# The first projection blocks of a transformer layer, put in written order, with four channel blocks of their modulation multiplied on TensorE

## The chip, the cores and the metric

The kernel runs on one core of a Trainium2 chip. The metric is the device time in microseconds (us) of one execution, from launch to the end on the chip; the time of a kernel is the median of its runs. A core has TensorE (PE in the rows), VectorE (DVE), ScalarE (ACT), GpSimd (POOL), a sequencer that issues transfers (SyncE, SP in the rows), and 16 DMA engines.

## The reference

One decoder layer on a sequence of 2048 positions with 1024 channels, in float32. A condition vector gives six vectors of 1024 numbers, the modulation; each sub-layer normalises its input, scales and shifts it by the modulation, and adds its result through a gate. Of what follows the projection only the names matter here: four heads of gated linear attention, eight heads of dilated attention, an output projection, a feed-forward part with a convolution of width 3.

```python
cond = jax.nn.silu(c)
mod = (cond @ w_ada[l] + b_ada[l])[:, None, :]
sh1, sc1, g1, sh2, sc2, g2 = jnp.split(mod, N_MOD, axis=-1)
h = rms_norm(x, norm1_g[l]) * (1 + sc1) + sh1
proj = h @ w_in[l]
gq, gk, gv, gr, glr, aq, ak, av = jnp.split(proj, split_at, axis=-1)
...
x = x + g1 * (mixed @ w_out[l])
h = rms_norm(x, norm2_g[l]) * (1 + sc2) + sh2
u = causal_depthwise_conv(h @ w_up[l], conv_w[l], conv_b[l])
x = x + g2 * ((jax.nn.silu(u_gate) * u_val) @ w_down[l])
```

## The kernel before

The sequence is worked in four chunks of 512 positions, the 1024 channels in eight blocks of 128, one on the partitions each. Every large product is done as three float32r matmuls (`mm3`): both factors are split into a high part and the rest, and high by high, high by rest and rest by high are added up in PSUM (lines 288, 289 and 290; which of the two factors is the stationary one depends on the product). Weights arrive by DMA as `wraw`; ScalarE rounds them to `whi` (line 226) and VectorE subtracts to get `wlo` (line 227). The normalised input `x` is multiplied by `G` and `rstd` on VectorE (line 415), ScalarE adds the shift and rounds to `hhi` (line 417), and VectorE forms `hlo` (line 419). `rstd` comes from a sum of squares: a matmul with a matrix of equal numbers (`ones`, line 402), then a logarithm and an exponential on ScalarE (`norm_end`).

The modulation is 48 blocks of 128 numbers. A block is one row of 1024 weights on each partition (`wada`, 512 KB), multiplied by the condition and added up along the row on VectorE (line 326); then the bias is added (line 332) and, for a scale, `G` is formed (line 336). Channel block k of the first input needs two of them, the scale 8+k and the shift k. The first 16 blocks are fetched and multiplied at the start; the other 32 by `ada_late`, between other work (line 355).

The start goes as follows. The input of chunk 0 is fetched, `rstd` is formed, and for each channel block k its two modulation blocks are multiplied and `h0[k]` is formed. The first four output blocks of the projection, `FIRST`, have a PSUM tile each, to which channel block k can be added as soon as `h0[k]` and the weights are there: 4 x 8 x 3 = 96 matmuls of 128x512. Then comes the projection's next block, V0 (moving rows 272 wide), and the rest in the order of `ORDER0`: `g0 g1 g2 g3 V0 q0 q1 W0 q2 q3 V1 q4 q5 q6 q7 W1`. W1 is a block of four `wide` steps; ScalarE and VectorE turn its four PSUM tiles into `stg` (lines 496 and 497), and `stg` frees the tiles. Weights for the later blocks, the late modulation and the statistics of the next chunk (`stats`: eight loads, squares and sums, then `norm_end`) are laced into the projection by counting steps (`along`), and the mixing of chunk 0 (`mix(0)`) starts 27 steps later. A compiler pass with a timeline of its own sorts each engine's instructions, so that the order on an engine is not that of the code where nothing pins it. Loads of constants, the input of chunk 1 and the late modulation wait for a chosen instruction (`gate_ins`, `after`), here the modulation of k = 6 (`GATE`).

Of the kernel before, what the change touches and what calls it, by code (L numbers as in the profile page):

```python
# [26 lines left out]
GATE = 6  # L27
# [103 lines left out]

class K:
# [19 lines left out]
    def cload(self, name, shape, dt=F32):  # L152
        t = self.const.tile(list(shape), dt, name=name + "_sb")
        self.nc.sync.dma_start(t, self.A[name])
        return t

# [18 lines left out]
    def consts(self):  # L175
        nc, A = self.nc, self.A
        self.ct = self.const.tile(list(CONSTS.shape), F32, name="consts_sb")
        self.after(nc.sync.dma_start(self.ct, A["consts"]))
        self.mk = self.cload("masks", MASKS.shape, U32)
# [6 lines left out]
        nc.vector.tensor_scalar(self.qgs, self.C("qsc"), self.qg[:, 0:1], -0.5, op0=ALU.mult, op1=ALU.mult)  # L186
        self.kgs = self.const.tile([P, 1], F32, name="kgs")
        nc.vector.tensor_scalar(self.kgs, self.kg, -0.5, None, op0=ALU.mult)
        self.gw = self.const.tile([17, 256], F32, name="gw")
        nc.sync.dma_start(self.gw[0:16], A["gla_w_gate"])  # L190
        nc.sync.dma_start(self.gw[16:17], A["gla_b_gate"])
        self.gB = self.const.tile([P, 4, P], F32, name="gB")
        g = A["gla_norm_g"]
        nc.sync.dma_start(self.gB, bass.AP(tensor=g.tensor, offset=g.offset, ap=[[0, P], [0, 4], [1, P]]))
        nc.vector.tensor_scalar(self.gB, self.gB, 0.5, None, op0=ALU.mult)
        self.blk = self.const.tile([P, P], F32R, name="blk")
        nc.vector.tensor_copy(self.blk, self.C("blk"))
# [95 lines left out]
    def ada_setup(self):  # L293
        nc, c = self.nc, self.A["c"]
        self.cond = self.const.tile([P, 1024], F32, name="cond")
        nc.sync.dma_start(self.cond, bass.AP(tensor=c.tensor, offset=c.offset, ap=[[0, P], [1, 1024]]))
        self.n1 = self.cload("norm1_g", [P, KD])
        self.n2 = self.cload("norm2_g", [P, KD])
# [30 lines left out]
    def ada_end(self, b):  # L329
# [3 lines left out]
        for j, G, g in ((1, self.G1, self.n1), (4, self.G2, self.n2)):  # L333
            if b // KD == j:
                k = b % KD
                nc.vector.scalar_tensor_tensor(G[:, k:k + 1], m, 1.0, g[:, k:k + 1], op0=ALU.add, op1=ALU.mult)
# [641 lines left out]

    def run(self):
        self.ada_setup()  # L980
        self.scratch()
        self.x1, self.h2, self.tail = {}, {}, ()
        self.planned = False
# [5 lines left out]
        for k in range(KD):  # L989
# [3 lines left out]
            for g in gs:  # L993
                next(g)
# [81 lines left out]
def colv(v):  # L1076
    return v.reshape(-1, P).T
# [37 lines left out]
```

## Time and profile before

| | us |
|---|---|
| median of 3 runs | 2643.39 |
| lowest and highest run | 2640.31, 2644.96 |
| the profiled execution, its own time | 2639.45 |
| span of the profiled execution, first to last instruction | 2637.7 |

The profiled execution took 1.75 us more than its span, and 3.94 us less than the median. Rows of the trace give times from the start of the span. In a row of a timeline the first number is the start of an instruction, the second its length; matmuls overlap, so that the distance of two starts is shorter than a length. In square brackets stands the idle time of the engine before it and what ended it.

### The profile page before, as it was taken

To read this page: it belongs to the slowest core of one execution; us is meant where nothing else is said; L and a number is where in the kernel's file an instruction comes from. 1 tells how busy PE (TensorE), PEld (TensorE's weight loads), DVE (VectorE), ACT (ScalarE), POOL (GpSimd) and SP (SyncE) were. 2 spreads that over 40 slices of the span, in tenths; PEclk is the share of its full clock that TensorE was granted. 3 is DMA by queue.
4 is the path that set the end of the run, shared out by engine and by line. 5 is a ranking of instruction groups with operands and counts; after the bars stand their busy time and mean duration, and the time that the engine had idled before them with its cause. 6 is when DMAs were issued, how large, how long until landed. Compare 5 with 4: busy or idle time off the path is not lost.

```text
span 2637.7 us, 46896 instructions
## 1 busy us (share of the span) xinstructions
PE 2575.8 (98%) x18152; PEld 2114.0 (80%) x18152; DVE 1921.7 (73%) x4120; ACT 1276.3 (48%) x2607; POOL 243.8 (9%) x460
## 2 busy tenths in 40 slices
PE   5999999999989999999999999999999999999999
PEld 4878888788768888888788888878888888788887
DVE  7577886758677776776887777778778766666665
ACT  4556556656445444553545445345455443433332
POOL 0111101101000000000000000000000000010010
PEclk9999999999989999999999999999999999999999
DMA  8766565756623343446434444643344445332222
GB/s 290 256 201 226 189 230 182 231 177 204 225 81 104 98 124 127 126 151 218 140 102 128 136 133 138 199 164 111 112 149 129 136 133 182 134 104 96 96 96 88
DMA packets 192640, 405.10 MB, mean 154 GB/s; under 512 B 19985, under 2 KB 70946, under 8 KB 191138
## 3 DMA queue, kind: packets, MB, share of 16 engines
q0 software_dynamic: 60992, 220.49, 25.8%
q1 hardware_dynamic: 131426, 181.62, 21.0%
q8 instruction: 143, 2.34, 0.4%
q14 instruction: 79, 0.65, 0.1%
HBM read 339.12 MB, written 62.91 MB: 152 GB/s over the span
## 4 chain that ended last, share of the span: by engine, by line
PE 88%; DVE 4%; DMA 4%; ACT 2%; issue 1%; SPq 0%; POOL 0%; DVEq 0%; ACTq 0%; POOLq 0%
PE psg L288 26%; PE psg L289 25%; PE psg L290 25%; PE psa L757 2%; PE psa L737 2%; PE psa L859 2%; DMA wada<-in_w_ada_dram 1%; PE psa L595 1%; DVE wlo L227 1%; DMA x<-x 1%; PE psa L773 1%; PE psa L854 1%; PE psa L666 1%; DMA sq<-in_xT_dram 1%; PE psa L665 1%
## 5 line engine op out<-in xcount | busy, mean ns | idle before, releaser
L288 PE MATMUL psg<-hhi,whi 128*128 128x512 f32 x2040 | 807.5, 398 | 16.5 <-ACT hhi L417 8.6
L289 PE MATMUL psg<-hlo,whi 128*128 128x512 f32 x2040 | 804.9, 395 | 2.4 <-DVE hlo L419 2.4
L290 PE MATMUL psg<-hhi,wlo 128*128 128x512 f32 x2040 | 803.6, 394 | 0.9 <-DVE wlo L227 0.9
L226 ACT CAST whi<-wraw 128x1024 fp32r<-128x1024 f32 (+1 forms) x391 | 410.3, 1050 | 492.7 <-PE psg L289 422.4
L227 DVE TENSOR_TENSOR wlo<-wraw,whi 128x1024 fp32r<-128x1024 f32 (+1 forms) x391 | 478.8, 1225 | 186.6 <-ACT whi L226 179.8
L288 PEld LDWEIGHTS psg<-hhi,whi 128*128 128x128 f32 x2040 | 386.0, 189 | 104.6 <-ACT hhi L417 10.7
L290 PEld LDWEIGHTS psg<-hhi,wlo 128*128 128x128 f32 x2040 | 385.9, 189 | 83.9 <-DVE wlo L227 2.1
L289 PEld LDWEIGHTS psg<-hlo,whi 128*128 128x128 f32 x2040 | 386.1, 189 | 83.6 <-DVE hlo L419 3.5
L288 PE MATMUL psg<-ghi,whi 128*128 128x512 f32 x704 | 279.6, 398 | 0.0
L289 PE MATMUL psg<-glo,whi 128*128 128x512 f32 x704 | 277.3, 394 | 0.0
L290 PE MATMUL psg<-ghi,wlo 128*128 128x512 f32 x704 | 276.1, 392 | 0.0
L971 DVE SCALAR_TENSOR_TENSOR x<-psg,mod,x 128x512 f32<-128x512 f32 x192 | 143.0, 749 | 118.0 <-PE psg L290 115.8
L220 POOL DMA_DIRECT2D wraw<-in_w_up_dram x176 | 93.0, 528 | 1077.2 <-DVE wlo L227 954.8
L288 PE MATMUL psg<-whi,hhi 128*128 128x512 f32 (+2 forms) x512 | 175.3, 345 | 9.4 <-DVE stg L497 6.8
L289 PE MATMUL psg<-wlo,hhi 128*128 128x512 f32 (+2 forms) x512 | 174.9, 342 | 0.0
L290 PE MATMUL psg<-whi,hlo 128*128 128x512 f32 (+2 forms) x512 | 173.5, 340 | 0.0
L288 PEld LDWEIGHTS psg<-ghi,whi 128*128 128x128 f32 x704 | 132.3, 188 | 31.8 <-issue 4.0
L290 PEld LDWEIGHTS psg<-ghi,wlo 128*128 128x128 f32 x704 | 132.3, 188 | 28.3 <-issue 1.2
L289 PEld LDWEIGHTS psg<-glo,whi 128*128 128x128 f32 x704 | 132.4, 188 | 27.9 <-issue 2.1
L747 ACT ACTIVATE big<-big,nm 128x256 f32<-128x256 f32 (+1 forms) x256 | 122.5, 481 | 49.2 <-DVE nm L762 49.0
L926 ACT ACTIVATE y<-psg,conv_b_sb,conv_w_sb 128x512 f32<-128x512 f32 x176 | 135.9, 774 | 5.5 <-PE psg L290 2.9
L928 DVE SCALAR_TENSOR_TENSOR y<-psg,conv_w_sb,y 128x510 f32<-128x510 f32 x176 | 131.1, 745 | 0.8
(207 smaller groups left out, 3404.2 us busy)
## 6 DMA issues: line engine op xcount, KB each, us to landing
wraw<-in_w_up_dram POOLq DMA_DIRECT2D x176, 512.0 KB, 3.6
wraw<-in_w_down_dram POOLq DMA_DIRECT2D x88, 512.0 KB, 3.6
wraw<-in_w_ch_dram POOLq DMA_DIRECT2D x44, 512.0 KB, 4.3
v<-v SPq DMA_DIRECT2D x68, 256.0 KB, 5.1
wada<-in_w_ada_dram POOLq DMA_DIRECT2D x64, 256.0 KB, 4.9
wraw<-in_w_tokw_dram POOLq DMA_DIRECT2D x32, 512.0 KB, 4.1
wraw<-in_w_out_dram POOLq DMA_DIRECT2D x32, 512.0 KB, 5.0
sq<-in_xT_dram SPq DMA_DIRECT2D x48, 256.0 KB, 4.3
```

Source lines behind the costliest of these rows:

```text
L220: (nc.gpsimd if self.planned else nc.sync).dma_start(raw[:, :n], src)
L226: nc.scalar.copy(hi[:, :n], raw[:, :n])
L227: nc.vector.tensor_tensor(lo[:, :n], raw[:, :n], hi[:, :n].bitcast(F32), op=ALU.subtract)
L288: nc.tensor.matmul(ps, wh, hh, start=first and k == 0, stop=False, skip_group_check=shared)
L289: nc.tensor.matmul(ps, wh, hl, start=False, stop=False, skip_group_check=shared)
L290: self.lastmm = nc.tensor.matmul(ps, wl, hh, start=False, stop=k == n - 1, skip_group_check=shared)
L737: nc.tensor.matmul(at(i, hh, z), q[H[hh], i * P:(i + 1) * P], key(H[hh], i, z), start=True, stop=True, skip_group_check=True)
L747: nc.scalar.activation(t[:, lo:hi], t[:, lo:hi], AF.Exp, bias=nm[:, hh, g, i:i + 1], scale=2.0 ** -(h + 1), accum_out=dn[:, hh, g, i:i + 1])
L757: nc.tensor.transpose(ps[:n, i * P:(i + 1) * P], part(S[hh], i), self.C("id"))
L926: nc.scalar.activation(y, ps, AF.Identity, bias=self.cb[:, b:b + 1], scale=self.cw[:, 2, b:b + 1])
L928: nc.vector.scalar_tensor_tensor(y[:, 2:], ps[:, :T - 2], self.cw[:, 0, b:b + 1], y[:, 2:], op0=ALU.mult, op1=ALU.add)
L971: nc.vector.scalar_tensor_tensor(x1, ps, self.mod[:, 40 + cb:41 + cb], x1, op0=ALU.mult, op1=ALU.add)
```

## The change

The start is written out in one function, `begin`, and each of its instructions on TensorE, VectorE, ScalarE and SyncE is held to the written order (`Pinned`; in a trace they all bear the helper's line 142). The modulation of channel blocks 2 and 3 (`u = 1`), and of 4 and 5 (`u = 2`), scale and shift, is multiplied on TensorE: the weights come as `w_ada1`, eight tiles of 128x512 for each `u`; `ada_rows` multiplies each of them with 32 equal columns of the condition as the stationary factor, four column groups of the array at a time, ScalarE copies the result out of PSUM, `ada_sum` turns it to the partitions with four matmuls of one column, and VectorE adds the bias and forms two columns of `G` at once. Blocks 0, 1, 6 and 7 stay on VectorE. The channel blocks are used in the order 0, 1, 2, 3, 6, 4, 5, 7. TensorE gets 36 matmuls of 128x128 on constants ahead of the sum for `rstd`, and 10 behind it. All loads of constants, the first loads of chunk 1 and the late modulation wait for the multiply of block 7 now, and four operations on constants (`const_ops`) stand seven steps into the projection. The loads of later weights are issued by GpSimd throughout. The statistics of the next chunk are paced over 16 steps of the projection instead of 18.

```diff
-GATE = 6
+WARM = 36
...
+    def const_ops(self):
+
+        nc = PinnedAll(self.tc)
+        nc.vector.tensor_scalar(self.qgs, self.C("qsc"), self.qg[:, 0:1], -0.5, op0=ALU.mult, op1=ALU.mult)
+        nc.vector.tensor_scalar(self.kgs, self.kg, -0.5, None, op0=ALU.mult)
+        nc.vector.tensor_scalar(self.gB, self.gB, 0.5, None, op0=ALU.mult)
+        nc.vector.tensor_copy(self.blk, self.C("blk"))
...
-        (nc.gpsimd if self.planned else nc.sync).dma_start(raw[:, :n], src)
+        nc.gpsimd.dma_start(raw[:, :n], src)
...
+    def ada_rows(self, u, raws):
+
+
+        ps = self.pa()
+        for k in range(KD):
+            j = k % 4
+            self.nc.tensor.matmul(ps[32 * j:32 * j + 32], self.crep[:, k], raws[k], start=k < 4, stop=k >= 4, skip_group_check=True)
+        t = self.tmp.tile([P, T], F32, name="sq", bufs=3)
+        self.nc.scalar.copy(t, ps)
+        return t
+
+    def ada_sum(self, u, t):
+
+        nc = self.nc
+        pm = self.pa()
+        for i in range(4):
+            nc.tensor.matmul(pm[:, i:i + 1], t[:, i * P:(i + 1) * P], self.sel, start=True, stop=True, skip_group_check=True)
...
+        warm(WARM)
...
+        ms = self.pa()
+        nc.tensor.matmul(ms, self.ones, acc, start=True, stop=True)
+        whi(0)
+        mul(KD)
+        mul(0)
...
+        wlo(0)
...
+        warm(10)
+        hmul(0)
+        mul(KD + 1)
+        hlo(0)
+        mul(1)
+        for i in range(4):
+            t = big()
+            load(t, self.A["w_ada1"][1, i])
+            rows[2] += [t[:, 0:T], t[:, T:]]
+        load(raw[3][:, 0:1024], wch(3))
+        whi(1)
+        hmul(1)
+        wlo(1)
+        hlo(1)
+        mm(0, 0, 1)
+        mm(1, 0, 1)
+        t = self.ada_rows(1, rows[1])
+        mul(KD + 6)
+        whi(2)
+        wlo(2)
+        scale(7, ([half("ghi"), half("glo")], [half("ghi"), half("glo")]))
+        self.ada_sum(1, t)
+        mm(2, 0, 1)
+        hmul(2)
+        hmul(3)
+        hlo(2)
+        mul(6)
+        hlo(3)
+        hmul(6)
+        for b in (0, 1, 2):
+            mm(b, 2)
+        t = self.ada_rows(2, rows[2])
+        whi(3)
+        for b in (0, 1, 2):
+            mm(b, 3)
+        self.ada_sum(2, t)
+        hlo(6)
+        wlo(3)
+        hmul(4)
+        hmul(5)
+        for b in (0, 1, 2):
+            mm(b, 6)
+        mm(3, 0, 1, 2, 3, 6)
+        hlo(4)
+        mul(KD + 7)
+        hlo(5)
+        for k in (4, 5):
+            for b in FIRST:
+                mm(b, k)
+        mul(7)
+        self.gate_ins = self.last
+        hmul(7)
+        hlo(7)
+        for b in FIRST:
+            mm(b, 7)
...
-            return along(stats(c), 11, proj(c - 1), 18)
+        def ahead(c, g):
+
+            return along(stats(c), 11, g, 16)
 
-        gemm = along(self.ada_late(), 66, chain(ahead(1), ahead(2), ahead(3), proj(3)), 98)
-        for _ in range(27):
+        first = proj(0)
+        for _ in range(7):
+            next(first)
+        self.const_ops()
+        gemm = along(self.ada_late(), 66, chain(ahead(1, first), ahead(2, proj(1)), ahead(3, proj(2)), proj(3)), 91)
+        for _ in range(20):
             next(gemm)
```

On TensorE at the start of the program, before the change, the sum for `rstd` (L402) comes first and the three kinds of `mm3` follow as the compiler pass sorted them:

```order
L402 MATMUL psa<-rstd,ones 128x512
L288 MATMUL psg<-hhi,whi 128x512 x2
L289 MATMUL psg<-hlo,whi 128x512
L290 MATMUL psg<-hhi,wlo 128x512
L288 MATMUL psg<-hhi,whi 128x512
```

After the change the constant matmuls stand around that sum:

```order
L142 MATMUL psa<-ones 128x128 x36
L142 MATMUL psa<-rstd,ones 128x512
L142 MATMUL psa<-ones 128x128 x10
L142 MATMUL psg<-hhi,whi 128x512
L142 MATMUL psg<-hlo,whi 128x512
```

Behind four groups of three stand the eight matmuls of `ada_rows` (out of `wada` and the condition `crep`) and the four of `ada_sum` (`sel` is the column of equal numbers):

```order
L142 MATMUL psg<-hhi,whi 128x512
L142 MATMUL psg<-hlo,whi 128x512
L142 MATMUL psg<-hhi,wlo 128x512
L142 MATMUL psa<-wada,crep 32x512 x8
L142 MATMUL psa<-sel,sq 128x1 x4
L142 MATMUL psg<-hhi,whi 128x512
L142 MATMUL psg<-hlo,whi 128x512
```

What moved: the modulation's multiplies are now between matmuls of the first four blocks, and the matmul behind `ada_sum` is the first of the third block.

On TensorE the sum of squares of chunk 1 (`psa<-rstd,ones`, L402 before) stood between block V1 (256 wide) and the matmuls of the next block of chunk 0:

```order
L289 MATMUL psg<-wlo,hhi 128x256
L290 MATMUL psg<-whi,hlo 128x256
L402 MATMUL psa<-rstd,ones 128x512
L288 MATMUL psg<-hhi,whi 128x512
L289 MATMUL psg<-hlo,whi 128x512
L290 MATMUL psg<-hhi,wlo 128x512
```

After the change (L466 now) it stands inside W1, 31 matmuls of 128x512 ahead of that block's last, beside the two of the last attention key block's norm (L510 and L511):

```order
L321 MATMUL psg<-wlo,hhi 128x512
L322 MATMUL psg<-whi,hlo 128x512
L510 MATMUL psa<-sqr,blk 128x512
L466 MATMUL psa<-rstd,ones 128x512
L320 MATMUL psg<-whi,hhi 128x512
L511 MATMUL psa<-sqr,blk 128x512
L321 MATMUL psg<-wlo,hhi 128x512
L322 MATMUL psg<-whi,hlo 128x512
```

What moved: the sum of squares of chunk 1, from V1's end into W1.

On VectorE, the rows ahead of W1's `stg` (the last row), before the change; L415 multiplies chunk 1's input by `G` and `rstd`:

```order
L419 SCALAR_TENSOR_TENSOR hlo<-sq,mod,hhi 128x512
L415 SCALAR_TENSOR_TENSOR sq<-sq,G_110,rstd 128x512
L227 TENSOR_TENSOR wlo<-wraw,whi 128x1024
L332 TENSOR_TENSOR mod<-mod,b_ada_sb 128x1
L355 ISA wada,mod<-wada,cond 128x512
L355 ISA mod 128x1
L579 COPY kt<-psa 128x512
L415 SCALAR_TENSOR_TENSOR sq<-sq,G_110,rstd 128x512
L606 TENSOR_TENSOR kt<-psa,consts_sb 128x128
L455 SCALAR_TENSOR_TENSOR stg<-stg,kgs,sq 128x512
L606 TENSOR_TENSOR kt<-psa,consts_sb 128x128
L497 SCALAR_TENSOR_TENSOR stg<-stg,psg 128x512 x4
```

After the change the first twelve of the same stretch, up to the four `stg` ones (L479 is the line of L415, L259 that of L227, L561 that of L497, L678 that of L614):

```order
L643 COPY kt<-psa 128x512
L441 SCALAR_TENSOR_TENSOR sq<-nwt,sq 128x512
L670 TENSOR_TENSOR kt<-psa,consts_sb 128x128
L479 SCALAR_TENSOR_TENSOR sq<-sq,G_171,rstd 128x512
L670 TENSOR_TENSOR kt<-psa,consts_sb 128x128
L396 TENSOR_TENSOR mod<-mod,b_ada_sb 128x1
L479 SCALAR_TENSOR_TENSOR sq<-sq,G_171,rstd 128x512
L259 TENSOR_TENSOR wlo<-wraw,whi 128x1024
L678 TENSOR_TENSOR pt<-kt 128x512
L519 SCALAR_TENSOR_TENSOR stg<-stg,kgs,sq 128x512
L479 SCALAR_TENSOR_TENSOR sq<-sq,G_171,rstd 128x512
L561 SCALAR_TENSOR_TENSOR stg<-stg,psg 128x512 x4
```

What moved: in this piece one more multiply of chunk 1's input (L479) and one product of the mixing (`pt`, L678) stand ahead of `stg`. Three more L479, in one row ("x3"), stand 14 rows ahead of the piece's first, and between that row and the piece the order has one weight rest (L259) more than before.

## Rows read from the trace of the kernel before

**Rows 1.** The page: the span, and TensorE's busy time, share and instructions.
```profile
span 2637.7 us, 46896 instructions
...
PE 2575.8 (98%) x18152; PEld 2114.0 (80%) x18152; DVE 1921.7 (73%) x4120; ACT 1276.3 (48%) x2607; POOL 243.8 (9%) x460
```

**Rows 2.** TensorE's waits, 0 to 64 us: waiter, releaser, us in total, times, longest.
```profile
PE psa L402 <- DVE rstd L396: 14.5, 1, 14.5
PE psg L288 <- ACT w L226: 4.8, 1, 4.8
PE psg L288 <- ACT hhi L417: 4.3, 1, 4.3
```

**Rows 3.** The chain that ends with the first V0 matmul: start us, length, piece.
```profile
12.60 7.80 DMA wada<-in_w_ada_dram
...
30.23 10.30 DMA wraw<-in_w_ch_dram
40.55 1.05 ACT w L226
```

**Rows 4.** Three stretches: us, PE, PEld, DVE, ACT, POOL busy (x), PEclk, DMA share, GB/s.
```profile
20.00:41.60 21.60, 10.44 (x21) 6.28 (x21) 18.68 (x48) 5.69 (x8) 1.07 (x2) 1.00 0.81 283
47.50:62.00 14.50, 14.20 (x63) 11.39 (x61) 10.38 (x24) 5.90 (x9) 1.48 (x3) 1.00 0.78 269
180.00:200.00 20.00, 14.17 (x120) 11.65 (x119) 20.00 (x35) 10.79 (x16) 3.15 (x5) 0.83 0.71 231
```

**Rows 5.** TensorE's timeline at the end of the first four blocks: start us, us, instruction.
```profile
46.51 0.63 PE L289 MATMUL psg<-hlo,whi 128*128 128x512 f32 x1
46.93 0.63 PE L290 MATMUL psg<-hhi,wlo 128*128 128x512 f32 x1
...
47.67 0.40 PE L289 MATMUL psg<-hlo,whi 128*128 128x512 f32 x1
47.90 0.40 PE L290 MATMUL psg<-hhi,wlo 128*128 128x512 f32 x1
...
62.32 0.40 PE L288 MATMUL psg<-whi,hhi 128*128 128x272 f32 x1 [0.62 <-ACT stg L472]
```

**Rows 6.** VectorE's timeline, 14 to 24 us: one of each kind.
```profile
16.30 1.23 DVE L227 TENSOR_TENSOR wlo<-wraw,whi 128x1024 fp32r<-128x1024 f32 x1 [0.23 <-ACT whi L226]
17.44 1.22 DVE L326 CUSTOM_DVE_ANT_0 wada<-wada,cond 128x1024 f32<-128x1024 f32 x1
...
21.88 0.75 DVE L415 SCALAR_TENSOR_TENSOR x<-x,G,rstd 128x512 f32<-128x512 f32 x1
```

**Rows 7.** DMA, 0 to 64 us in 40 slices: GB/s moved.
```profile
GB/s 0 266 199 303 337 378 407 401 421 390 401 408 402 396 389 399 377 339 200 298 55 41 44 247 397 424 420 376 358 122 154 394 377 341 374 300 109 201 182 164
```

**Rows 8.** Timelines of TensorE for full-precision and 32-column matmuls.
```profile
14.52 2.08 PE L402 MATMUL psa<-rstd,ones 128*128 128x512 f32 x2 [14.52 <-DVE rstd L396]
...
134.07 1.02 PE L402 MATMUL psa<-rstd,ones 128*128 128x512 f32 x2
...
2107.17 0.47 PE L288 MATMUL psg<-hhi,whi 128*128 128x512 f32 x1
2107.58 1.10 PE L854 MATMUL psa<-v,s 128*32 128x64 f32 x64
```

**Rows 9.** End of chunk 0's block W1: the wait, then timelines of VectorE, ScalarE, TensorE.
```profile
PE psg L288 <- DVE stg L497: 5.8, 1, 5.8
...
176.06 0.75 DVE L375 SCALAR_TENSOR_TENSOR nwt<-psa,eps,sq 128x512 f32<-128x512 f32 x1 [4.27 <-ACT sq L452]
...
187.15 2.48 DVE L497 SCALAR_TENSOR_TENSOR stg<-stg,psg 128x512 f32<-128x512 f32 x4
...
175.39 0.63 ACT L452 ACTIVATE sq<-sq 128x512 f32<-128x512 f32 x1
...
180.54 0.39 PE L290 MATMUL psg<-whi,hlo 128*128 128x512 f32 x1
...
187.89 0.80 PE L288 MATMUL psg<-whi,hhi 128*128 128x512 f32 x1 [5.83 <-DVE stg L497]
```

More of the change, by code (lines that the diff above doesn't have):

```diff
@@ L129, in chain, with __init__, __getattr__, call @@
         yield from g
+class Pinned:
+    def __init__(self, tc, eng):
+        self.tc, self.eng = tc, eng
+    def __getattr__(self, name):
+        f = getattr(self.eng, name)
+        def call(*a, **kw):
+            r = f(*a, **kw)
+            self.tc.keep_in_program_order(r)
+            return r
+        return call
+class PinnedAll:
+    def __init__(self, tc):
+        for e in ("tensor", "vector", "scalar", "sync"):
+            setattr(self, e, Pinned(tc, getattr(tc.nc, e)))
 class K:
@@ L153, in cload, with gated @@
         t = self.const.tile(list(shape), dt, name=name + "_sb")
-        self.nc.sync.dma_start(t, self.A[name])
+        self.gated(self.nc.sync.dma_start(t, self.A[name]))
         return t
+    def gated(self, ld):
+        if self.gate_ins is not None:
+            self.after(ld)
     def C(self, name):
@@ L294, in ada_setup @@
         nc, c = self.nc, self.A["c"]
+        col = self.cload("c_col", [P, KD])
         self.cond = self.const.tile([P, 1024], F32, name="cond")
@@ L332, in ada_end @@
         nc.vector.tensor_tensor(m, m, self.ba[:, b:b + 1], op=ALU.add)
[L333 to L336, printed above, removed]
+        if b // KD in (1, 4):
+            G, g = (self.G1, self.n1) if b // KD == 1 else (self.G2, self.n2)
+            k = b % KD
+            nc.vector.scalar_tensor_tensor(G[:, k:k + 1], m, 1.0, g[:, k:k + 1], op0=ALU.add, op1=ALU.mult)
     def ada_late(self):
@@ L979, in run @@
     def run(self):
-        self.ada_setup()
         self.scratch()
         self.x1, self.h2, self.tail = {}, {}, ()
-        self.planned = False
-        xs = self.load_x(0)
-        rstd = {0: self.norm_stats(lambda k: xs[k])}
-        h0, ws, done = [], {}, {b: self.pg() for b in FIRST}
-        spare = self.at.tile([P, 2048], F32R, name="w0", tag="kt", bufs=2)
-        ring = self.at.tile([P, 2048], F32, name="ring", tag="kt", bufs=2)
-        for k in range(KD):
-            big = [self.at.tile([P, 1024], F32, name="wada", tag="big", bufs=4)]
-            pair = [self.gp.tile([P, T], F32, name="wada", tag=t) for t in ("ghi", "glo")] if k < 5 else [ring[:, k % 2 * 1024:k % 2 * 1024 + 1024]]
-            gs = [self.ada(KD + k, big), self.ada(k, pair)]
-            for g in gs:
-                next(g)
-            if k < len(FIRST):
-                b = FIRST[k]
-                ws[b] = self.wblock(self.A["w_ch"][b], KD, P, spare if k == 3 else None)
-            for g in gs:
-                next(g, None)
-            if k == GATE:
-                self.gate_ins = self.last
-            h0.append(self.norm_mod1(xs[k], k, rstd[0], self.G1, self.mod[:, 0:8]))
@@ L1003, in run @@
-        for b in FIRST:
-            for k in range(KD):
-                self.mm3(done[b], ws[b][k:k + 1], h0[k:k + 1], k == 0, True)
+        done, rstd, h0 = self.begin()
         self.consts()
@@ L1039, in stats @@
             yield
-        def ahead(c):
-            return along(stats(c), 11, proj(c - 1), 18)
-        gemm = along(self.ada_late(), 66, chain(ahead(1), ahead(2), ahead(3), proj(3)), 98)
-        for _ in range(27):
+        def ahead(c, g):
[6 more added lines that the diff above has]
+        for _ in range(20):
             next(gemm)
```

114 lines of the change are left out of this document (101 added, 13 removed).

## The prediction

> **What bounds the kernel now.** I read the page first. TensorE is busy 2575.8 of 2637.7 us [rows 1], so about 62 us are to be had from it without taking work away. The view of its waits for the first 64 us shows where nearly half of them lie: 14.5 us until the sum of squares can start, later 4.8 us for the fourth weight block (`w`) and 4.3 us for `hhi` [rows 2]. The reader should see that none of these is a wait for TensorE's own speed. The chain that ends with the first V0 matmul says what stands behind them: transfers of `wada`, then the transfer of the fourth `wraw`, issued at 30.23 us and landed at 40.53, then ScalarE's rounding, then matmuls without a gap to 62.32 us [rows 3, 5]. The windows add that between 20 and 41.6 us TensorE is busy 10.44 of 21.60 us, and VectorE, with the modulation, 18.68 [rows 4].
>
> The other half of the story is TensorE's clock. Up to 46.93 us two matmuls of 128x512 start 0.42 us apart, which is the 1.2 GHz level; from 47.67 us on 0.23 us apart, the 2.4 GHz level [rows 5]. The 96 matmuls of `FIRST` would take 96 x 0.23 = 22 us at the upper level; the window from 47.5 to 62 us has 63 matmuls [rows 4], so about a third of the 96 ran at the lower one.
>
> The third view is the wait at the end of chunk 0's W1. TensorE's last matmul of W1 starts at 180.54 us and the next block starts at 187.89 us, after 5.83 us idle that VectorE's `stg` (L497) ends [rows 9]. VectorE had been idle for 4.27 us up to 176.06 and then worked without a break to 187.15, when `stg` came [rows 9]: 11.09 us of queued work.
>
> **The start, after the change.** Bytes first. The first modulation block lands at about 12.6 us (a new piece of the chain begins there [rows 3]), and from 9 to 25 us the transfers run at 377 to 421 GB/s [rows 7]; at about 400 a block of 512 KB takes 1.3 us. In the order written on SyncE that gives estimated landings of 15.2 us for the first weights, 19.1 for the second, 24.3 for the eight tiles of `u = 1`, 25.6 for the third weights, 28.2 for channel block 6's modulation, 34.8 for the tiles of `u = 2` (with one weight block that GpSimd fetches between), 36.1 for the fourth weights, 38.7 for block 7's modulation. The fourth weights land 4.4 us before those of today.
>
> Then VectorE and ScalarE in written order, with 1.22 us (multiply), 1.2 (`wlo`), 0.7 (`x`, `hlo`) [rows 6]: two multiplies for block 0 end at 15.3, `rstd` is there at 17.6, `x` and `hhi` of block 0 at 19.2 (its first matmul now starts at 20.86: the idle row in front of it is the 4.3 us of [rows 2]), the pair of block 1 with its rest at 24.1. Twelve matmuls end at 26.1, `ada_rows` at 28.0, its copy and `whi` of block 2 at 29.8, `wlo` at 31.1; the rest of blocks 2 and 3 at 35.4, `ada_rows` for `u = 2` at 37.4, `hlo` of block 6 at 41.0. From there nothing waits any more: block 7's `hlo` is ready at about 50.1, and its twelve matmuls come last. Behind 41.0 us stand 60 matmuls: 9 for block 6 with the first three weight blocks, 15 for the fourth weights with blocks 0 to 3 and 6, 24 for blocks 4 and 5, 12 for block 7; by 0.23 that is 13.8 us. So `FIRST` ends at 54.8 us if the clock is at its upper level from 24 us on.
>
> The matmuls on constants are meant to have it there, but the 5.5 us from the sum of squares to the first `hhi`, and the pauses up to 33 us, can lose it. Today it came only in the long run behind ScalarE's `w` at 41.6 us [rows 3, 5], and it was lost again around the 5.8 us pause of W1 (the window from 180 to 200 us has a mean clock of 0.83 [rows 4]). If the first twelve matmuls and the first `ada_rows` go at the lower level (12 x 0.2 + 2 = 4.4 us more, of which waits for weights hide a part), the end is about 57.5 us. I take 56.7, nearer to that. V0 follows 0.6 us later, as now: 57.3 instead of 62.32, **5.0 us gained**; bounds 2 (level back at 40 us) and 7.5. The Trainium skill (TensorE: Matmul & The Clock Gate, HAM oscillation) describes bursts of matmuls between waits, each of which runs at the lower clock. By that rule the pauses of the new start would keep the level low through most of it, and the end would be 61.8 us or later instead of 56.7, which is the second rival. The trace agrees for the old start: 0.42 us spacing until 46.93 us, after pauses up to 41.6 [rows 3, 5].
>
> The parts of this: VectorE loses eight multiplies, 8 x 1.3 = 10.4 us with their small rows; that is what lets the pairs of blocks 2 to 5 come without waiting in its queue. TensorE gains the two `ada_rows`. A full-precision matmul of 128x512 takes 1.02 us at the upper level, 2.08 at the lower [rows 8]. Eight of 32 columns take 8 x 1.02 = 8.2 us one after another, and 2 x 1.02 = 2 us if four column groups run together. The trace has an instruction of that kind: 64 records of 32 columns by 64 in 1.10 us [rows 8], where a record of 512 is half of 1.02 us, so that 64 of 64 columns one after another would take 64 x 0.51 / 8 = 4.1 us. So groups do run together, about four at a time, and I take 2 us each. The 46 constant matmuls lie in the 14.5 us and the 4.3 us in which TensorE waits anyway [rows 2]; a quarter of 1.02 or 2.08 us each, 36 take 9 us at the upper level and at most 19 at the lower, and only if the level stays low for all of them do they push the sum of squares back, by up to 6 us. `ada_sum` (four one-column matmuls) and ScalarE's two copies of some 0.6 us are in the chain above.
>
> Changing from whole-array matmuls to four column groups and back happens four times. The one such change in the rows costs 0.41 us from start to start where 0.23 is usual [rows 8], so 4 x 0.2 = 0.8 us. They are inside the 56.7.
>
> **What comes back at W1.** The statistics of chunk 1 are paced over fewer steps that are left, so their sum of squares has moved from V1's end into W1, 31 matmuls before the last. With 31 x 0.23 = 7.1 us to W1's end (T0, when the matmul behind the last could start), less 1.0 for the sum and 1.3 for two ScalarE rows of 0.63 [rows 9], `rstd` of chunk 1 is there at T0 - 4.8. In VectorE's queue the three multiplies that need it stand first, and all that is ahead of `stg` behind them. Before, the same queue began at 176.06 us, T0 - 4.7 with T0 = 180.54 + 0.23, and held 11.09 us. Now it holds four multiplies of chunk 1's input, one weight rest and one product of the mixing more: 4 x 0.66 + 1.14 + 0.62 = 4.4 us. So `stg` starts at T0 - 4.8 + 15.5 = T0 + 10.7 instead of T0 + 6.4, and the wait grows from 5.8 to about 10.1 us: **4.3 us lost**. Bounds: 0, if VectorE gets some of this done in the 4.27 us that it now idles (the sum could land earlier in the chain than I place it), and 8, if the other waits in that stretch slip too. What TensorE waits for behind it has the same order again from about 700 us on; the short waits between W1 and there may move by one or two either way, which I set to 0.
>
> **The sum.** 2639.45 - 5.0 + 4.3 = 2638.8 for an execution like the profiled one. The median stands 3.9 us above that one, so I forecast 2642.7 us: no change that a measurement of this kernel can tell, which ends at about 0.2%, or 5.3 us.
>
> **Rivals.**
> *The wait at W1 does not grow.* VectorE does the moved multiplies in its idle time, or the sum lands earlier. Then only the start counts: 2643.4 - 5.0 = 2638.4, down to 2635 with the clock up from 24 us. For it: 4.27 us of idle time right ahead of the queue. Against: that idle time ends with ScalarE's row for the norm, and the moved multiplies wait for `rstd`, which comes no sooner.
> *The clock stays at 1.2 GHz through the start (slower).* TensorE's stream stays broken by waits until 33 us, as it is now until 41.6, and now the lower level lasts to 47 us [rows 5]. If the level is never back before V0, the 96 matmuls take 41 us and the two `ada_rows` 8, and with hardly a wait from 20 us on the end is about 69; V0 is 7 us late, and with W1 the time is 2654.7. With the level back at 45 us the end is about 61.8, V0 is where it was, and W1's loss alone gives 2647.7. So it decides from about 45 us on. The matmuls on constants fill the longest pause, which speaks against it.
> *Column groups run one after another (slower).* Then `ada_rows` takes 8.2 us twice, `FIRST` ends near 64.6, V0 is 2.9 us late, and the time 2650.6. Against it: the 64 records of [rows 8].
> *The start doesn't gain at all.* TensorE's part is shorter, but the transfers are as many as before; if they run behind the estimated landings by 5 us, V0 is where it was, and W1's loss stands: 2647.7. For it: 283 GB/s in the stretch 20 to 41.6 us [rows 4], well below 400; but that mean holds three slices from 32 to 37 us with 41 to 55 GB/s [rows 7], behind a stop for buffers that VectorE's modulation had to free, and eight of its multiplies are gone.
>
> **Numbers.** Chances: the forecast 0.42; W1's wait not longer 0.33; clock low 0.10; groups in a row 0.06; no gain at the start 0.09. Of the second case about 0.24 is beyond 0.2%, with 0.06 of the forecast's better side (a start gain of 7.5 and a small loss): faster 0.30. Slower: the clock case, the groups, a third of the last case and the forecast's worse side, 0.20 in all. The rest, 0.50, is the same. The range leaves out only the far clock case and the best start with no loss: 2634 to 2650; the forecast's own range is 2638 to 2648.
>
> **What would show it.** Right: V0's first matmul near 57.3 us, 0.23 us spacing from about 30 us; `ada_rows` in about 2 us; the wait of L561 at W1 near 10 us, with six multiplies of chunk 1's input ahead of `stg`. Wrong: 0.42 us spacing beyond 40 us; two 8 us stretches of `wada`; a wait at W1 of 6 us or less, when the time is 5 us lower; a wait of SyncE on `mod` of several us again.

## The result, and the profile after

The changed kernel is slower by 0.29%, 7.5 us, and the twenty runs of each tell that from no change.

| | before | after |
|---|---|---|
| median of 20 runs, us | 2639.49 | 2647.01 |
| lowest and highest | 2636.52, 2644.96 | 2643.39, 2652.66 |
| ratio, 95% interval | | 1.0029 (1.0023 to 1.0035) |
| span of the profiled execution, us | 2637.7 | 2641.7 |

The profiled execution of after is one of its quickest, so its span shows 4.0 of the 7.5 us. The page of after, where TensorE's busy time has grown by 16.7 us, most of it the matmuls on constants:

```profile
PE 2592.5 (98%) x18292; PEld 2127.0 (81%) x18292; DVE 1911.0 (72%) x4092; ACT 1276.0 (48%) x2610; POOL 244.9 (9%) x460
```

TensorE's waits of after, first 0 to 64 us and then 64 to 300 us (waiter, releaser, us in total, times, longest):

```profile
PE psg L142 <- ACT hhi L142: 3.2, 3, 2.0
PE psg L142 <- DVE hlo L142: 3.0, 4, 1.5
PE psa L142 <- DVE rstd L142: 2.9, 1, 2.9
```

```profile
PE psg L320 <- DVE stg L561: 9.4, 1, 9.4
PE psa L608 <- ACT gl L592: 3.1, 2, 2.1
PE psg L320 <- ACT stg L564: 1.7, 1, 1.7
```

The start did get its waits removed: 14.5 us for the sum of squares are 2.9, and the fourth weights [rows 2] are gone from the list. But behind it stand a wait of 9.4 us at W1, where 5.8 were [rows 9], and one for `gl` that the kernel before does not have. `gl` is a narrow result of V0, copied out of PSUM by ScalarE; L608 turns it on TensorE right behind V0.

TensorE's timeline of after: the constants, two of the first matmuls, one `ada_rows`, the wait ahead of block 6's `hlo`, two matmuls behind it, the first V0 matmul. A matmul on full-precision numbers leaves two records, so x72 are the 36.

```profile
1.07 9.95 PE L142 MATMUL psa<-ones 128*128 128x128 f32 x72 [1.07 <-DVE ones L142]
...
14.97 3.95 PE L142 MATMUL psa<-ones 128*128 128x128 f32 x20
...
25.77 0.63 PE L142 MATMUL psg<-hhi,whi 128*128 128x512 f32 x1
26.20 0.63 PE L142 MATMUL psg<-hlo,whi 128*128 128x512 f32 x1
...
28.46 1.92 PE L142 MATMUL psa<-wada,crep 128*32 128x512 f32 x16
...
44.83 0.50 PE L142 MATMUL psg<-hlo,whi 128*128 128x512 f32 x1 [1.49 <-DVE hlo L142]
...
45.72 0.63 PE L142 MATMUL psg<-hlo,whi 128*128 128x512 f32 x1
46.15 0.63 PE L142 MATMUL psg<-hhi,wlo 128*128 128x512 f32 x1
...
59.98 0.28 PE L320 MATMUL psg<-whi,hhi 128*128 128x272 f32 x1
```

V0 starts at 59.98 us instead of 62.32 [rows 5]: the start gains 2.3 us. `ada_rows` takes 1.92 us, so the column groups do run together. Matmuls at 25.77 and 26.20 us are still 0.43 us apart, the 1.2 GHz level. From 33.71 to 42 us those that follow one another are 0.23 us apart, the 2.4 GHz level (granted clock 1.00 between 30 and 45 us); behind the wait for block 6's `hlo` eight are 0.43 us apart again (45.41 to 48.71 us, granted clock 0.66 between 45 and 50), which costs some 8 x 0.2 = 1.6 us. The windows of after (us, PE, PEld, DVE, ACT, POOL busy, PEclk, DMA share, GB/s) answer to [rows 4]:

```profile
20.00:41.60 21.60, 16.20 (x75) 8.85 (x75) 12.44 (x24) 7.02 (x10) 0.66 (x1) 0.84 0.87 336
...
180.00:200.00 20.00, 10.60 (x103) 8.65 (x102) 20.00 (x35) 11.93 (x18) 2.92 (x6) 0.74 0.66 200
```

VectorE is busy 12.44 us instead of 18.68 between 20 and 41.6 us, TensorE 16.20 instead of 10.44. Around W1 the mean clock is 0.74, where it was 0.83.

W1's end in after: VectorE's queue from the multiplies of chunk 1's input to `stg`, then TensorE.

```profile
178.51 2.08 DVE L479 SCALAR_TENSOR_TENSOR sq<-sq,G,rstd 128x512 f32<-128x512 f32 x3 [4.59 <-ACT rstd L469]
...
193.98 2.47 DVE L561 SCALAR_TENSOR_TENSOR stg<-stg,psg 128x512 f32<-128x512 f32 x4
...
194.71 0.80 PE L320 MATMUL psg<-whi,hhi 128*128 128x512 f32 x1 [9.40 <-DVE stg L561]
```

That queue is 193.98 - 178.51 = 15.47 us long; the prediction had 15.5.

The new wait, on ScalarE and TensorE, 68 to 77 us:

```profile
71.94 0.63 ACT L455 ACTIVATE sq<-sq 128x512 f32<-128x512 f32 x1 [1.75 <-DMA sq<-in_xT_dram]
...
72.73 0.18 ACT L592 COPY gl<-psg 128x16 f32<-128x16 f32 x1
...
74.01 0.19 ACT L592 COPY gl<-psg 128x16 f32<-128x16 f32 x1
75.61 0.63 ACT L455 ACTIVATE sq<-sq 128x512 f32<-128x512 f32 x1 [1.40 <-DMA sq<-in_xT_dram]
...
76.39 0.18 ACT L592 COPY gl<-psg 128x16 f32<-128x16 f32 x1
...
74.26 0.28 PE L608 MATMUL psa<-consts_sb,gl 128*16 128x128 f32 x1 [1.02 <-ACT gl L592]
76.62 0.38 PE L608 MATMUL psa<-consts_sb,gl 128*16 128x128 f32 x1 [2.09 <-ACT gl L592]
...
77.23 0.63 PE L321 MATMUL psg<-hlo,whi 128*128 128x512 f32 x1
77.66 0.63 PE L322 MATMUL psg<-hhi,wlo 128*128 128x512 f32 x1
```

The reader should see `sq` (L455, a square of chunk 1's input for its statistics) wait 1.40 us for its transfer at 75.61 us, the third of four copies of `gl` behind it at 76.39, and TensorE's L608 at 76.62 after 2.09 us idle. Seven matmuls behind that go 0.43 us apart (77.23 to 77.66): the level fell in the wait. Together 3.1 + 7 x 0.2 = 4.5 us. SyncE's timeline shows why the squares are late, in after and then in before:

```profile
52.01 0.33 SPq L205 DMA_DIRECT2D consts_sb<-in_consts_dram  x1
...
58.13 0.41 SPq L220 DMA_DIRECT2D gB<-in_gla_norm_g_dram  x1
58.58 2.61 SPq L1209 DMA_DIRECT2D sq<-in_xT_dram  x3
61.28 4.19 SPq L537 DMA_DIRECT2D gq<-stg  x2
65.56 4.46 SPq L537 DMA_DIRECT2D gk<-stg  x2
70.11 0.41 SPq L1209 DMA_DIRECT2D sq<-in_xT_dram  x1
```

```profile
50.20 0.33 SPq L178 DMA_DIRECT2D consts_sb<-in_consts_dram  x1
50.58 9.34 SPq L1011 DMA_DIRECT2D sq<-in_xT_dram  x6
```

Both hold back the large load of constants (`consts_sb`) until a late modulation block is done, at 52.01 and 50.20 us. Before, chunk 1's input follows at once, six loads from 50.58 us. After, nine small loads of constants (`gB` is the last) stand between, so that its first load is issued at 58.58 us, 1.4 us ahead of V0 instead of 11.7, and the fourth at 70.11, behind the stores of `gq` and `gk`, which SyncE also takes in order. The issue is only one part of the delay. The loads of chunk 1's input also take longer from issue to landing (number of loads, KB each, median us), in after (52 to 75 us), before (0 to 64) and d0 (54 to 72), a run below in which the nine loads stand elsewhere:

```profile
sq<-in_xT_dram SPq DMA_DIRECT2D x5, 256.0 KB, 10.0
```

```profile
sq<-in_xT_dram SPq DMA_DIRECT2D x7, 256.0 KB, 4.4
```

```profile
sq<-in_xT_dram SPq DMA_DIRECT2D x9, 256.0 KB, 4.4
```

`gB`, the last of the nine, takes 9.7 us to land, and between 60 and 65 us the DMA engines move 35 GB/s. Why the loads land so late is not shown. Between 40 and 84 us ScalarE's squares wait 13.8 us for their transfers, the longest 7.1, where before they wait 5.7.

### The profile page after: what moved, and what is told of

It is laid out like the page before. It is cut to its first block, busy times and chain, and to the rows that moved or that the text cites. A ratio compares the mean times of both kernels' runs of the same rounds, so it can differ in the third digit from the quotient of the medians.

```text
span 2641.7 us, 47144 instructions
## 1 busy us (share of the span) xinstructions
PE 2592.5 (98%) x18292; PEld 2127.0 (81%) x18292; DVE 1911.0 (72%) x4092; ACT 1276.0 (48%) x2610; POOL 244.9 (9%) x460
## 4 chain that ended last, share of the span: by engine, by line
PE 81%; DVE 2%; DMA 2%; ACT 1%; issue 0%; SPq 0%; DVEq 0%; ACTq 0%
PE psg L320 23%; PE psg L321 23%; PE psg L322 23%; PE psa L801 3%; PE psa L821 3%; PE psa L923 2%; PE psa L659 1%; PE psa L837 1%; PE psa L918 1%; DMA qf<-q 0%; PE psa L730 0%; PE psa L729 0%; PE psa L938 0%; DVE x L1035 0%; PE psa L734 0%
## 5 line engine op out<-in xcount | busy, mean ns | idle before, releaser
L320 PE MATMUL psg<-hhi,whi 128*128 128x512 f32 x2016 | 795.0, 396 | 8.8 <-ACT hhi L481 4.4
L321 PE MATMUL psg<-hlo,whi 128*128 128x512 f32 x2016 | 792.2, 393 | 0.2 <-DVE hlo L483 0.2
L322 PE MATMUL psg<-hhi,wlo 128*128 128x512 f32 x2016 | 790.7, 393 | 1.0 <-DVE wlo L259 1.0
L259 DVE TENSOR_TENSOR wlo<-wraw,whi 128x1024 fp32r<-128x1024 f32 (+1 forms) x388 | 474.4, 1223 | 187.9 <-ACT whi L258 182.7
L320 PEld LDWEIGHTS psg<-hhi,whi 128*128 128x128 f32 x2016 | 379.7, 189 | 93.8 <-ACT hhi L481 4.9
L322 PEld LDWEIGHTS psg<-hhi,wlo 128*128 128x128 f32 x2016 | 379.6, 188 | 81.6 <-issue 1.8
L321 PEld LDWEIGHTS psg<-hlo,whi 128*128 128x128 f32 x2016 | 379.9, 188 | 79.6 <-issue 3.1
```

Of the source, the lines that this page charges most:

```text
L259: nc.vector.tensor_tensor(lo[:, :n], raw[:, :n], hi[:, :n].bitcast(F32), op=ALU.subtract)
L320: nc.tensor.matmul(ps, wh, hh, start=first and k == 0, stop=False, skip_group_check=shared)
L321: nc.tensor.matmul(ps, wh, hl, start=False, stop=False, skip_group_check=shared)
L322: self.lastmm = nc.tensor.matmul(ps, wl, hh, start=False, stop=k == n - 1, skip_group_check=shared)
```

## The experiments

Medians and ratios are against the kernel before on the same chip; effects are differences of ratios, as the median of before moved between 2636.9 and 2639.5 us from chip to chip.

| run | median us | ratio (95% interval) |
|---|---|---|
| the changed kernel | 2647.0 | 1.0029 (1.0023 to 1.0035) |
| a1 gate on block 6 | 2649.1 | 1.0038 (1.0024 to 1.0052) |
| a2 faster pace | 2642.3 | 1.0011 (1.0001 to 1.0022) |
| a3 a1 and a2 | 2643.0 | 1.0014 (1.0006 to 1.0023) |
| a4 no constant matmuls | 2647.5 | 1.0032 (1.0020 to 1.0043) |
| a5 input behind `gl`, pace | 2640.7 | 1.0003 (0.9994 to 1.0011) |
| a6 input behind `gl` | 2646.4 | 1.0025 (1.0015 to 1.0036) |
| a7 blocks 2 to 5 on VectorE | 2652.4 | 1.0048 (1.0036 to 1.0060) |
| a8 squares late, pace | 2638.6 | 0.9997 (0.9989 to 1.0006) |
| a9 V0's weight rest late | 2644.3 | 1.0027 (1.0018 to 1.0037) |
| a10 a8 and a9 | 2639.3 | 1.0004 (0.9995 to 1.0012) |
| b1 before, gate on block 7 | 2637.2 | 0.9993 (0.9985 to 1.0002) |
| b2 before, pace of the change | 2652.0 | 1.0041 (1.0028 to 1.0055) |
| c1 small loads free | 2646.2 | 1.0037 (1.0024 to 1.0051) |
| c2 c1, pace | 2639.8 | 1.0008 (0.9999 to 1.0017) |
| c3 c2, weight rest late | 2639.4 | 1.0007 (0.9999 to 1.0016) |
| d0 small loads behind `gl` | 2640.6 | 1.0010 (1.0001 to 1.0019) |
| d1 d0, pace | 2636.5 | 0.9996 (0.9988 to 1.0005) |
| d2 d1, weight rest late | 2635.7 | 0.9991 (0.9982 to 0.9999) |

**W1's wait (a2, b2).** The pace of chunk 1's statistics, in the changed kernel:

```diff
-            return along(stats(c), 11, g, 16)
+            return along(stats(c), 11, g, 9 if c == 1 else 16)
```

> The changed kernel with chunk 1's statistics paced over 9 of the 11 steps that are left instead of 16, so that their sum of squares stands about where it stood before. Theory A (the sum of squares inside W1 brings chunk 1's multiplies ahead of stg on VectorE): W1's wait falls from 9.4 to 5 or 6 us, the gl waits stay, and the time falls by about 4 us, to 2643. Theory B: W1's wait may fall, but a later wait takes it up, and the time stays within 1.5 us of 2647.0.

In b2 the kernel before takes seven steps of the projection without the statistics and then paces them over 16, as in the change's diff.

> The kernel before, with the pacing of the changed one alone (seven steps without chunk 1's statistics, then 16). Theory A: the sum of squares stands 30 matmuls before W1's end as in the changed kernel, W1's wait grows from 5.8 to about 9.5 us, and the time rises by about 4 us to 2643.5. Theory B: within 1.5 us of 2639.5.

TensorE's waits of a2, then of b2, from 64 and from 40 us on:

```profile
PE psg L320 <- DVE stg L561: 5.8, 1, 5.8
PE psa L608 <- ACT gl L592: 3.4, 1, 3.4
```

```profile
PE psg L288 <- DVE stg L497: 9.6, 1, 9.6
PE psg L288 <- ACT w L226: 3.2, 1, 3.2
PE psg L288 <- ACT stg L472: 3.1, 1, 3.1
PE psg L288 <- ACT stg L500: 2.9, 1, 2.9
```

The wait is 5.8 us where the sum of squares stands ahead, 9.4 to 9.6 where it stands inside W1, in either kernel. a2 takes 0.18% off, 4.7 us, as expected. b2 adds 0.41%, 10.8 us, far more than the 4 expected and than its 3.8 us at W1: its squares also came ahead of V0's copies on ScalarE (`stg` L472, 3.1 us) and a third wait follows W1 (L500, 2.9). That the pace costs about what W1's wait grows by is shown by a2; b2 moved more than one thing. The 1.7 us for ScalarE's `stg` (L564), which followed W1's wait in after, are gone in a2 too.

**The gate and the squares (a1, a3, b1, a5, a6, a8).** a1 moves `self.gate_ins = self.last` from behind `mul(7)` to behind `mul(6)`; a3 adds a2's edit.

> The changed kernel with one line moved: the loads of constants and of chunk 1's input wait for the multiply of block 6 instead of block 7. Theory A (the late loads put chunk 1's squares ahead of gl on ScalarE, so TensorE waits 1.0 + 2.1 us for gl behind V0 and then runs seven matmuls at the lower level): the two waits for gl vanish, W1's wait stays near 9.4 us, and the time falls by about 3.1 + 1.5 = 4.6 us from 2647.0 to about 2642.4. Theory B (the loss is the start itself, or what is saved there is given back at later waits): the time stays within 1.5 us of 2647.0.

> Both edits, the earlier gate and the faster pace, in the changed kernel. Theory A: the two losses add up, 4.6 + 4 us, so about 2638.4, slightly under the kernel before (2639.5), by less than the start's gain of 2.3. Theory B: above 2644.

Both missed. The waits for `gl` went, as expected, and two for `hhi` came in the first four blocks. ScalarE in a1:

```profile
52.06 0.63 ACT L455 ACTIVATE sq<-sq 128x512 f32<-128x512 f32 x1 [9.78 <-DMA sq<-in_xT_dram]
53.05 0.63 ACT L455 ACTIVATE sq<-sq 128x512 f32<-128x512 f32 x1 [0.35 <-DMA sq<-in_xT_dram]
53.58 0.70 ACT L142 ACTIVATE hhi<-x,mod 128x512 fp32r<-128x512 f32 x1
```

A square that waits 9.78 us for its transfer now stands ahead of `hhi` of block 4, whose `x` VectorE has ready at 46.3 us: `hhi` starts 7 us later than it could, and V0 at 68.92 us. The squares cost where they stand in ScalarE's order ahead of what TensorE needs next.

b1 sets `GATE = 7` in the kernel before.

> The kernel before with GATE 7 instead of 6: constants and chunk 1's input are loaded one channel block later. Theory A: squares of chunk 1 stand between the gl copies on ScalarE as in the changed kernel, TensorE waits for gl behind V0 for 2 to 4 us, and the time rises by 3 to 5 us, to about 2643.5. Theory B: the squares don't matter, the time is within 1.5 us of 2639.3.

It missed too: no wait for `gl`, no loss. A gate on block 7 alone is not the cause. a6 lets chunk 1's input wait for V0's last copy of `gl`, a5 adds the pace; a8 holds the squares back instead, behind the gate's last logarithm, with the pace. The edit of a6:

```diff
-                if c == 1:
-                    self.after(ld)
+                if c == 1:
+                    self.tc.add_manual_dep(ld.ins, self.glcopy.ins.name, ...)
```

> The changed kernel with chunk 1's input loaded only behind V0's last copy of gl, its own pace. Theory A: the waits for gl vanish without a new one in the first four blocks, W1's wait stays at 9.4 us, and the time is 2647.0 - 3.1 - 1.5 = about 2642.4. Theory B: within 1.5 us of 2647.0.

> The changed kernel with the faster pace of a2, and with chunk 1's input loaded only behind V0's last copy of gl, so that no square of chunk 1 stands ahead of a gl copy on ScalarE. Theory A (squares that wait for their transfer hold up what stands behind them on ScalarE: gl in the changed kernel and in a2, hhi in a1 and a3): no wait for gl or for hhi, W1's wait 5.8 us, time 2642.3 - 3.4 - 1.5 = about 2637.4, so 2 us under the kernel before. Theory B (a saving ahead of 700 us is given back at later waits and by the clock there): 2641 or more.

> The changed kernel with the faster pace of a2, and with chunk 1's squares (not their loads) held behind the gate's last logarithm on ScalarE, so that neither gl on ScalarE nor glr on VectorE has a square ahead of it. Theory A (a square that waits for its transfer stalls what is queued behind it): no wait for gl and none for glr, W1's wait 5.8 us, time 2642.3 - 3.4 - 1.5 = about 2637.4. Theory B (whatever is saved there is given back at another wait): 2640.5 or more.

TensorE's waits of a6 and of a8:

```profile
PE psa L615 <- DVE glr L611: 3.1, 1, 3.1
```

```profile
PE psa L512 <- ACT sqr L506: 2.7, 2, 2.1
PE psa L513 <- DVE sqr L507: 1.6, 2, 0.8
```

In a6 the square no longer holds up ScalarE's `gl`, but VectorE's `glr` (L611) stands behind the copy of that square, and TensorE waits 3.1 us there: nothing won. a5, with the pace, has the same wait (2.2 us) and is 0.08% under a2, within the noise. In a8 a wait for the norm of the first attention block follows (2.7 + 1.6 us, where after has 0.6 + 0.8). Even so a8 is 0.14% under a2, 3.7 us, at the edge of the noise, and level with the kernel before, near its theory A. So the edits of a1 and a6 moved the wait and won nothing; holding the squares back seems to win, though its trace shows new waits nearly as long as the one that went, and why is open.

**The nine small loads (c1, d0).** c1 takes them out of the gate; d0 puts them behind V0's first copy of `gl`, five steps into the projection.

> The changed kernel with the nine small loads of constants no longer held behind block 7's multiply; only the large one and chunk 1's input still are. Theory J (the nine loads put chunk 1's input 6 us later on SyncE, so its squares arrive late on ScalarE): its first load is issued at about 52.5 us instead of 58.6, the wait for gl falls from 3.1 us to 1 or less, W1's wait stays at 9.4, and the time falls by 3 to 4.6 us from 2647, to 2642.5 to 2644. Theory K (the loads are late for the stores of gq and gk and the three buffers between them, and the nine loads don't matter, or cost as much ahead of the modulation): within 1.5 us of 2647.

> The changed kernel with its nine small loads of constants moved behind V0's first copy of gl, so that chunk 1's input stands right behind the large constant load on SyncE, as before the change. Theory J (the nine loads make chunk 1's squares late): its first load is issued near 52.5 us, no wait for gl or glr above 1 us, V0 stays near 60 us, W1's wait 9.4 us, time 2647 - 4.6 = about 2642.5. Theory L (the squares wait in any case, since V0 comes earlier and their transfers don't): another wait of 2 us or more between 50 and 110 us, time 2645 or more.

```profile
PE psa L142 <- DMA wada<-in_w_ada_dram: 5.3, 1, 5.3
```

```profile
54.46 0.33 SPq L205 DMA_DIRECT2D consts_sb<-in_consts_dram  x1
54.83 7.21 SPq L1214 DMA_DIRECT2D sq<-in_xT_dram  x5
```

In c1 the wait for `gl` is gone, but the nine are now ahead of the modulation's tiles for blocks 4 and 5, and TensorE waits 5.3 us for `wada`; nothing is won (1.0037). In d0 five loads of chunk 1 follow the large constant load at once, no wait for `gl` or `glr` is left, W1's wait is 9.4 us, and 0.19% comes off, 5.0 us. In its profiled execution V0 starts late, at 63.0 us, with more matmuls 0.43 us apart and a wait of 0.5 us for a `stg` behind a square; that alone would give the transfers more time. But in d2 below, with the nine loads in the same place, V0 starts at 60.58 us and there is no wait for `gl` or `glr` either. So the nine loads, where the change put them, were the second loss.

**What is left with both mended (d1, d2, c2, c3, a9, a10).** a9 holds the rest of V0's first weights (`wlo`, L259) behind `mul(7)`; the others combine edits as the table says.

> The changed kernel with the rest of V0's first weights (wlo, L259) held behind block 7's multiply on VectorE, nothing else. Theory E (that instruction, which waits 3.98 us for ScalarE's whi, holds up hlo of block 6 from 41 to 44 us and is why the start gains 2.3 and not 5): the wait for hlo of 1.5 us vanishes, V0 starts 2.5 to 3 us earlier, at 57 to 57.5, and the time falls to about 2644.3. Theory F (the start is bound elsewhere, by transfers or the clock): V0 at 59.5 or later.

> a8 and a9 together: faster pace, squares held back, V0's weight rest held back. If the three losses are separate and all of it, V0 starts near 57.3, no wait behind V0, W1's wait 5.8 us, and the time is 2637.4 - 2.7 = about 2634.7, some 4 us (0.16%) under the kernel before. If they are given back later: 2638 or more.

> c1 with the faster pace of a2. Theory J: no wait for gl above 1 us, W1's wait 5.8 us, and the start's gain of 2.3 us is what is left: 1 to 3 us under the kernel before, near 2636.5. Theory K: as a2, 2642.

> c2 with the rest of V0's first weights held behind block 7's multiply as in a9. Theory J: V0 near 58 us and the time about 1.5 us under c2. Theory K: as c2 or above.

> d0 with the faster pace of a2. Theory J: W1's wait 5.8 us and the time about 2638, 1 to 2 us under the kernel before on the same chip. Theory L: 1 us or more above it.

> d1 with the rest of V0's first weights held behind block 7's multiply. Theory J: V0 near 58 us, time 1 to 2 us under d1, 3 us under the kernel before. Theory L: as d1.

VectorE of after, ahead of block 6's `hlo`:

```profile
42.56 1.29 DVE L259 TENSOR_TENSOR wlo<-wraw,whi 128x1088 fp32r<-128x1088 f32 x1 [3.98 <-ACT whi L258]
...
44.03 0.74 DVE L142 SCALAR_TENSOR_TENSOR hlo<-x,mod,hhi 128x512 fp32r<-128x512 f32 x1
```

L259 waits 3.98 us for ScalarE, and `hlo` (44.03), whose own inputs are there by 39.4, stands behind it. In a9 TensorE's wait for that `hlo` is 0.8 us instead of 1.5, since the bias of blocks 4 and 5, which waits for `ada_sum` on TensorE, still stands ahead of it. The matmuls behind the wait are 0.23 us apart, and V0 starts at 58.15. The ratio is 0.02% lower, 0.5 us, which the intervals do not separate from nothing; and in a10 and d2, with the same edit and the same 0.8 us, V0 starts at 60.26 and 60.58, as other stretches went 0.43 us apart there. d1 has both losses mended: 0.33% under the changed kernel, 8.7 us, and level with the kernel before; a wait of 1.6 us for a `stg` behind a square is left ahead of V0. d2, with the third, is 0.09% under the kernel before, and its interval excludes no change, if narrowly, as one of eighteen such comparisons. c2, c3 and a10 are level with the kernel before: what they mend is paid elsewhere, in c2 and c3 by more than 5 us for `wada`, in a10 by waits as in a8 (1.6 + 1.6 us for the norm, 1.0 for `gl`).

**TensorE's part (a7, a4).** a7 multiplies blocks 2 to 5 on VectorE again, with the same bytes; a4 leaves out both `warm` calls.

> The changed kernel with channel blocks 2 to 5 of the modulation back on VectorE (the same bytes in the same order, no ada_rows, no ada_sum). Theory C (the multiplies on TensorE are what shortens the start): VectorE has eight multiplies more in its chain, 10.4 us, of which its idle time in the start hides a part; V0 starts 3 to 8 us later than 59.98, and the time rises by as much, to 2650 or more. Theory D (the written order alone shortens it, or the start is bound by the transfers): V0 within 1 us of 59.98, time within 1.5 us of 2647.

> The changed kernel without the 46 matmuls on constants. Theory G (they keep TensorE's clock at the upper level for part of the start): the sum of squares takes 2.1 instead of 1.25 us, matmuls stay 0.42 us apart until 28 us or later, V0 starts 1 to 3 us later, and the time rises to 2648 to 2650. Theory H (the pauses behind them lose the level again, so they bring nothing): V0 within 0.7 us of 59.98, time within 1.5 us of 2647.

V0 starts at 65.1 us in a7, 5.1 us later than in after and 2.8 later than before, and the time is 5 us higher (five runs, of which the profiled one is the slowest). So the multiplies on TensorE are worth about 5 us, and this written order without them would have been slower than the compiler's. In a4 V0 starts at 59.97 us, as in after: the 46 matmuls on constants bring nothing that can be measured. TensorE's first wait there, of 14.3 us, ends with the sum of squares, which starts at 14.3 us instead of 13.9. That sum takes 2.08 us instead of 1.25 and the matmuls go at the lower level until 27.7 us, as theory G had it, but the waits for `hhi` hide it:

```profile
PE psa L142 <- DVE rstd L142: 14.3, 1, 14.3
PE psg L142 <- ACT hhi L142: 5.5, 3, 3.4
```

## Why the prediction was wrong

It said 2642.7 us, no change; the kernel is 0.29% slower. The forecast stands on the median of three runs, 3.9 us above the profiled execution. The median of twenty, 2639.49 us, is level with that execution, so what was forecast is a change of -0.7 us, and what came is +7.5. That 2647.0 lies only 4.3 us from 2642.7 is luck. Nor is 0.2% the least that can be told: the interval of twenty runs is 0.06% to either side.

1. *W1's wait: right.* Queue 15.47 us for 15.5, wait 9.40 for 10.1, loss by a2 4.7 us for 4.3.
2. *The start: right in kind, half in size.* 2.3 us for 5.0, inside the bounds of 2 and 7.5. `ada_rows` took 1.92 us for 2, but began at 28.46 us and not at 26.1, since the matmuls ahead of it went 0.43 us apart (25.34 to 27.90 us); the 1.9 us between 54.8 and 56.7 allowed for much of that. The term mis-sized is `hlo` of block 6, which I had at 41.0 us and which is done at 44.8, since V0's weight rest stands ahead of it on VectorE and waits for ScalarE. Behind that wait eight matmuls go at the lower level once more. In a9 both shrink and V0 starts 1.8 of the missing 2.7 us earlier, but a10 and d2 did not repeat it, and its time shows no gain beyond the noise.
3. *The step that failed: the path of TensorE from V0 to W1, which the sum takes as unchanged.* The prediction set to 0 the short waits between W1 and 700 us; for those between V0 and W1 it has no term at all, and gives no reason. The diff moved nine loads of constants, which the kernel before issues between 22 and 30 us, all but one, behind the gate, ahead of chunk 1's input, and I priced the bytes of the modulation but not these loads on SyncE's queue. These loads made the squares late, by the issue (6.2 us) and by the landing (10.0 us behind the issue for 4.4); the squares made `gl` late, and TensorE paid 3.1 us of waiting and 1.4 us of slower matmuls behind V0; d0 gives 5.0 us back. The trace of before had the sign: ScalarE's squares wait 5.7 us for their transfers there too (40 to 84 us), but the copies of `gl` behind them (the first three at 69.5 to 72.0 us) were done before TensorE came to use them at 74.5. The Trainium skill (TensorE: Matmul & The Clock Gate, Architectural detail) says that ScalarE and VectorE take their queues strictly in order. The runs agree: in a1 `hhi` started 7 us behind its `x`, as a square ahead of it waited 9.78 us for its transfer, and in a6 the copy of a square held up `glr`.
4. *The rivals.* "The start doesn't gain at all" gave 2647.7, near the result by the same luck and for a wrong reason: it stands for a loss of 4.3 us, and the transfers were where I had them (the wait for block 6's modulation ends at 28.79 us, for 28.2). W1's wait did grow, and column groups did not run one after another. The clock did not stay low through the start, but the 0.43 us spacing beyond 40 us, a sign of being wrong, came for 3.3 us.

So: -2.3 at the start, +4.5 to 5.0 behind V0, +4.2 at W1 (3.6 of wait, ten matmuls at the lower level instead of seven) make 6.4 to 6.9, for 7.5 measured. That these are close is partly chance: the two profiled executions, from which the terms are read, differ by 4.0 us only. Between 60 and 300 us TensorE's waits grow from 7.1 to 16.1 us, the 1.7 for `stg` (L564) among them; from 300 us on they fall from 21.8 to 17.5.

What stays open: why the median execution loses 3.6 us more than the profiled one, and how much of the spread of the changed kernel's runs (2643.4 to 2652.7 us) is the clock in the start. Between profiled executions of d0 and after, which have the same start but for the small loads, V0 differs by 3 us with longer runs of 0.43 us spacing in d0; more was not tried.

## What to carry to other kernels

When a change puts loads behind a gate, list every load on that queue between the gate and the next load that an engine waits for; nine small loads took 6.2 us of SyncE's queue (52.38 to 58.58), and a chunk's input, issued that much later, also landed 10.0 us behind its issue instead of 4.4. An engine that takes its work in order turns one late operand into a wait of everything behind it: moving the gate (a1) or the input (a6) only chose which of TensorE's inputs stood behind. A gain at one place is worth looking for at the next wait: here 2.3 us came in and about 9 us went out at two waits further on, and with both mended (d1) the time is level with the kernel before, so that the start's gain itself stands in the traces and not yet in the times.

## What the runs showed of the hardware that was not expected

Matmuls on constants kept TensorE busy for 9.95 us and then 3.95, and the product matmuls from 25.77 us on still went 0.43 us apart, behind a pause of 2.0 us for `hhi`; leaving the constants out changed neither V0's start (59.97 us) nor the time (1.0032 against 1.0029). The Trainium skill (TensorE: Matmul & The Clock Gate, HAM oscillation) has bursts of matmuls between waits run at the lower clock. The trace of after agrees for the burst behind that pause and for the one behind block 6's 1.5 us; the matmuls from 33.71 to 42 us, between pauses of 0.3 to 0.6 us, went 0.23 us apart. Here filling one long pause did not help, as others of 1.5 and 2.0 us were left behind it.

Nine loads of 0.5 to 256 KB slowed the loads behind them on SyncE's queue as well as delaying their issue. In the seven runs that have the nine right ahead of chunk 1's input and square it at once (after, a1, a2, a3, a4, a7 and a9), its first square starts 9.7 to 10.0 us behind the issue of its load; in before, b1, b2, c1 to c3 and d0 to d2 it is 4.4 to 6.4 us. Which of the nine does it, and how, was not tried.
